# A two-layer encoder trunk on one core: the scaling of the turned queries, two units later in the written order

## The chip, the cores and the metric

The kernel runs on one core of one Trainium2 chip. The metric is the device time of one execution in microseconds; a kernel is run several times and the median counts. One execution is also recorded by the hardware profiler, and that record is the trace that is read here.

## What is computed

The trunk has a batch of 1, 256 rows (frames), a width of 2048, 16 heads of 128 and two layers, all in float32. The part around the change is layer a's attention. Cut to that, the reference reads:

```python
u = rms_norm(h, a_norm_g[l])
proj = u @ a_w_in[l]                                   # 2048 -> 3*2048 + 16
q, k, v, fz = jnp.split(proj, [D, 2 * D, 3 * D], axis=-1)
q = rms_norm(q.reshape(B, S, H, Dh), a_q_g[l])
k = rms_norm(k.reshape(B, S, H, Dh), a_k_g[l])
logf = jax.nn.log_sigmoid(fz + a_b_f[l])
o = forgetting_attention(q, k, v, logf)                # causal softmax with a decay bias
h = h + o.reshape(B, S, D) @ a_w_out[l]
h = h + sq_relu_mlp(h, mlp_norm_g[layer], mlp_w1[layer], mlp_w2[layer])
```

A shared key and value projection, a second layer with chunked attention (layer b) and a second MLP follow.

## The kernel before

Every large product is made of units. A unit takes a weight tile of 128 x 1024 numbers, which ScalarE (ACT) and VectorE (DVE) split in two: line 339 writes the high part `hi`, line 340 the rest `lo`. TensorE (PE) then does three passes: `hi` with the high part of the activations (line 608), `hi` with their low part (line 610) and `lo` with the high part (line 612). Weights come either as loaded tiles (`raw`, line 310, and the tiles called `R`, `h` and `w`) or as sums of two of them (`wT`), since pairs of panels share seven products in place of eight. Some pairs of layer a are 1536 columns wide; the 512 that are over are split into `half` by the same two lines. A `hi` tile has three buffers, so ACT can be at most a few units ahead of PE.

The projection of layer a runs by four groups g of four heads: queries, keys and values of a group one after the other. When the query panel of a group is done, its rows are normed and turned, so that a head's 128 numbers lie across the partitions:

- `head_norm` (line 666): ACT squares (676), DVE sums (679, 683), POOL takes the power -1/2 (684), ACT scales the rows by it (`qn`, 690) and DVE transposes blocks of 32 x 32 into `z` (456).
- `carry` (line 459): one DMA writes `z` to DRAM (`turn`, 466), four DMAs read it back with blocks exchanged (472). For the queries of the second to fourth group POOL issues the four; for the keys SP issues them, into the half tile called `R`.
- `scale_q` (line 708): one ACT instruction (711) reads the landed tile (`z`, 128 x 1024), multiplies by a gain for each partition and writes `q` in the layout that the scores use.

The keys go the same way without the last step. `attend` (783) then puts the softmax of each head into the order: scores on PE (744, 745: `po<-R,q`), exponentials on ACT (757), the probabilities turned through DRAM (`pbuf`), values on PE (776, 777), and the result split by ACT (780) and DVE (781).

What comes when on an engine is set by the order in which the program is written. `keep_order` chains the instructions of each engine in the written order, and each engine takes them strictly in turn. Work beside the units stands in a queue, `fill`: `add_fill` appends a list of items, one slot for each coming unit, and `run_fill` executes one slot, mostly once for each unit (a table of masks says 0, 1 or 2). An empty list in front of an item so puts it one slot later. `of_q` is called once for each group when the query panel is finished, and adds `scale_q` that many slots behind.

Words in the rows: `acc` and `s` are pairs of PSUM tiles; line 1042 and line 1052 copy or negate one of them on ACT between the forms of a pair (`p<-s`, `s<-s`), and line 1046 copies another; line 990 makes a summed weight tile on DVE; line 1005 adds one weight tile to another by a DMA from POOL.

Of the kernel before, what the change touches and what calls it, by code (L numbers as in the profile page):

```python
# [102 lines left out]
def trunk(ctx: ExitStack, tc: tile.TileContext, xT, xr, gs, hg, bf, wgate, w_in, w_in3, w_ins, w_oa, w1a, w1fa, w1sa, w2fa, w2sa,  # L103
# [340 lines left out]
    def steps(make):  # L444
        box = []

        def step():
            if not box:
                box.append(make())
            next(box[0])  # L450
        return step
# [34 lines left out]
    def turned(name=None):  # L486
        z = qkv.tile([P, GH * T], F32, name="z")
        return (z, qkv.tile([P, GH * T], F32, name=name, tag=name, bufs=2)) if name else z
# [177 lines left out]
    def head_norm(stats, z, dst, late=0, apart=None, reader=SY):  # L666

        rest = []

        def f(b, ps):  # L670
            sq = wk.tile([P, 512], F32, name="sq", tag="wk")
            ss = sm.tile([P, 3 * GH], F32, name="ss")
            rn = ss[:, GH : 2 * GH]

            def square():
                S.activation(sq, ps, AF.Square)

            def total():
                V.tensor_reduce(ss[:, :GH], sq.rearrange("p (a d) -> p a d", a=GH), axis=AX.X, op=ALU.add)

            def norm():
                vv = ss[:, 2 * GH :]
                V.tensor_scalar(vv, ss[:, :GH], 1.0 / P, stats().e[:, b : b + 1], op0=ALU.mult, op1=ALU.add)
                G.tensor_tensor(rn, vv, mhalf, op=ALU.pow)

            def turn():
                qn = wk.tile([P, 512], F32, name="qn", tag="wk")
                for a in range(GH):
                    c = slice(a * P, a * P + P)
                    S.activation(qn[:, c], ps[:, c], AF.Copy, scale=rn[:, a : a + 1])  # L690
                blocks32(qn, z, b)

            if apart is None:
                square()
            rest.append((square, total, norm, turn))
            if b == NB - 1:
                turns = [[t] for _, _, _, t in rest] + carry(z, dst, 1, reader)
                if apart is not None:
                    add_fill([[]] * apart + [[s, t, n] for s, t, n, _ in rest] + turns)
                    return  # L700
                for _, total, norm, _ in rest:
                    total()
                    if not late:
                        norm()
                add_fill([[]] * (late - 1) + ([[n for _, _, n, _ in rest]] if late else []) + turns)
        return f

    def scale_q(land, layer, g):
        tag = "qs"[g // 2 if layer else 0]
        q = qkv.tile([P, GH, T], F32, name="q", tag=tag, bufs=2)  # L710
        S.activation(q.rearrange("p a (b i c) -> p (a b) i c", b=NB, i=4),
                     land.rearrange("p (i ab c) -> p ab i c", i=4, c=32), AF.Copy, scale=gqk[:, layer : layer + 1])
        return q
# [56 lines left out]
    def free(g):  # L770
        assert g < 2 or set(range(g * GH - 2 * GH, g * GH - GH)) <= served, "rooms in use"
# [11 lines left out]
    def attend(g, q, k, v, decay, o, make_bias):  # L783
        st = [{} for _ in range(GH)]
        box = {}
        k4 = k.rearrange("p (i a b c) -> p a b i c", i=4, a=GH, b=NB)
        *at, far = TABLES["ATA" if decay else "ATB"][g]
        items = [[] for _ in range(at[-1] + far + 1)]
        step = steps(lambda: make_bias(g, box))
        for i in (5, 8, 9) if decay and g == 0 else (3, 6, 7):  # L790
            items[i].append(step)
        for a in range(GH):
            step = steps(lambda a=a: softmax(st[a], g, a, q(), k4, box["b"]))
            for i in range(4):
                items[at[a] + i].append(step)
            items[at[a] + 3].append(lambda a=a: add_fill(st[a]["carry"]))
            items[at[a] + far].append(lambda a=a: values(st[a], a, v, o, g * GH + a))
        return items

    def v_evac(v, r):  # L800
        def f(b, ps):
            S.activation(v[:, b, :], ps, AF.Copy, scale=r[:, b : b + 1])
        return f

    def add_fill(items):
        for i, it in enumerate(items):
            if i < len(fill):
                fill[i] = fill[i] + it
            else:
                fill.append(it)  # L810
# [29 lines left out]
    def rows_in(i):  # L840
        here.add(i)
        b, n = chunks[2 * i]
        c = slice(n * 512, n * 512 + UN)
        SY.dma_start(h[b][:, c], xr[b][:, c])
# [164 lines left out]
    def prepare(p, d):  # L1009
        if d == p.units[1] and "11 half" in p.has:  # L1010
            p.has.remove("11 half")
            SY.dma_start(p.t["11"][:, UN : p.cols], p.big["11"][:, UN : p.cols])
        if p.deep and d == p.units[4] - 1:
            make(p, "T3", 1)
        for name, at in zip(("12", "22", "21", "11", "T3", "T1"), p.units):
            if d == at and p.deep and name == "T3":
                make(p, "T3", 0)
            elif d == at:
                (bring if name[0] != "T" else put if p.adds and name == "T1" else make)(p, name)
# [117 lines left out]
    def sub(tag):  # L1137
        if tag not in halves_of:
            halves_of[tag] = room(tag, "R")
        return halves_of[tag]  # L1140
# [45 lines left out]
    def heads(out):  # L1186
        o, fs, qs, vs = [None] * H, [], {}, {}

        def of_q(g):
            box = []  # L1190

            def f(b, ps):
                if b == 0:
                    z, lq = turned("z")
                    box.extend((head_norm(lambda: st0, z, lq, 0 if g else 6, None, G if g else SY), lq))
                box[0](b, ps)
                if b == NB - 1:
                    add_fill([[]] * (7 + (0 if g else 6)) + [[lambda: qs.update({g: scale_q(box[1], 0, g)})]])
            return f

        def of_k(g):
            box = []

            def f(b, ps):
                if b == 0:
                    free(g)
                    box.append(sub(f"k{g % 2}")[:, : GH * T])
                    box.append(head_norm(lambda: st0, turned(), box[0]))
                    vs[g] = sub(f"v{g % 2}")[:, :UN].rearrange("p (b c) -> p b c", b=NB)
                box[1](b, ps)  # L1210
                if b == NB - 1:
                    add_fill(attend(g, lambda: qs[g], box[0], vs[g], True, o, decay_bias))
            return f

        def of_v(g):
            return lambda b, ps: v_evac(vs[g], st0.r)(b, ps)

        evacs = [f(g) for g in range(NG) for f in (of_q, of_k, of_v)]
        box = [13]

        def after():
            prepare(plan_h[0][0], box[0])
            box[0] -= 1

        panels(x, evacs[:1], begin, after)
        step = steps(head_gains)
        add_fill([[step], [], [], [], [step]])
        add_fill([[lambda: rows_in(3)]])
        add_fill([[lambda i=i: enter(i)] for i in range(8 - TABLES["RI"][3], 8)])
        fill[TABLES["RI"][3] - 1].append(st0.roots)  # L1230
        add_fill([[]] * TABLES["GS"][0] + gates(x, st0))
        step = steps(lambda: sum_x(fs))
        for i in TABLES["XS"]:
            add_fill([[]] * i + [[step]])
        panels(x, evacs[1:2], None, after, tail=tail_h)
        base = turns[0]

        last = next(p for p, q, i in plan_h[::-1] if isinstance(p, Pair) and p.order == "three")
        step3 = steps(lambda: sum_third(x, fs))
        add_fill([[]] * TABLES["X3"] + [[step3]] * 4)  # L1240
        run(plan_h, opener(x, fs, evacs, o, out, base, last, TABLES["XOH"], True), TABLES["HM"], plan_a[0][0])
        halves_of.clear()
        owner.clear()
# [21 lines left out]
    qs, evs = [], []  # L1265
    for g in range(NG):
        box = {}

        def f(b, ps, box=box, g=g):
            if b == 0:  # L1270
                z, lq = turned("z")
                box["lq"], box["f"] = lq, head_norm(lambda: st2, z, lq, apart=0 if g else None)
            box["f"](b, ps)
            if b == NB - 1:
                add_fill([[]] * (9 if g else 7) + [[lambda: qs.append(scale_q(box["lq"], 1, g))]])
# [146 lines left out]
```

## Time and profile before

| | |
|---|---|
| three runs | median 2060.13 us (2053.63 to 2060.47) |
| the profiled execution | 2058.26 us, of which the span of the trace is 2056.5 us |
| granted TensorE clock | 1.000 over the span |
| PE busy | 2044.3 us (99%) |
| DVE, ACT, POOL busy | 1784.8, 1409.1, 259.6 us |
| DMA | 560.92 MB, mean 273 GB/s |

The span is what the trace covers; 1.8 us of the execution lie around it. Busy time of PE is nearly the whole span, so what can be saved without leaving work out is the time in which PE stands still or follows late. An idle time in brackets in a timeline row stands ahead of that row's instruction on its engine, and the name behind the arrow is what it waited for.

### The profile page before, as it was taken

Reading aid. Unit: us, or ns where it says so; the run is one execution under the profiler, and the core shown is the slowest. Engines: PE = TensorE matmul, PEld = TensorE weight load, DVE = VectorE, ACT = ScalarE, POOL = GpSimd, SP = SyncE. Lnnn points to the kernel's source line nnn. Section 1 sums busy time; section 2 is a strip of 40 time slices with the busy share of each in tenths; the row PEclk is TensorE's granted clock in tenths of the full one; section 3 lists DMA queues with packets and bytes.
Section 4 is the critical chain, followed back from the end, with each engine's and each line's share of the span. In section 5 each row is a group of like instructions: output and inputs, shape, how many; then the busy total and the mean of one; then the engine's idle time right before and its main releaser. Section 6 shows DMA issues by size and latency. Waiting matters only on the chain.

```text
span 2056.5 us, 27163 instructions
## 1 busy us (share of the span) xinstructions
PE 2044.3 (99%) x9048; PEld 1684.9 (82%) x9048; DVE 1784.8 (87%) x2099; ACT 1409.1 (69%) x1826; POOL 259.6 (13%) x371
## 2 busy tenths in 40 slices
PE   9999999999999999999999999999999999999999
PEld 8778878878888888888888888888888888888887
DVE  7788887899899899899888788889988988988996
ACT  7666666677676677676778666667766676776764
POOL 1122110021101102101012111100111111111020
PEclk9999999999999999999999999999999999999999
DMA  8898998898888898898989988888988888888985
GB/s 324 268 286 268 303 294 243 296 280 259 295 265 278 262 296 277 235 291 274 263 252 290 290 256 273 262 267 280 291 290 259 272 265 297 254 288 257 299 260 150
DMA packets 176749, 560.92 MB, mean 273 GB/s; under 512 B 40912, under 2 KB 67936, under 8 KB 154080
## 3 DMA queue, kind: packets, MB, share of 16 engines
q1 hardware_dynamic: 153824, 464.47, 64.0%
q0 software_dynamic: 22496, 94.42, 23.5%
q8 instruction: 71, 1.16, 0.2%
q14 instruction: 70, 0.57, 0.1%
q10 hardware_dynamic: 288, 0.30, 0.0%
HBM read 519.22 MB, written 27.29 MB: 266 GB/s over the span
## 4 chain that ended last, share of the span: by engine, by line
PE 88%; DMA 5%; DVE 3%; issue 2%; ACT 2%; POOL 0%; SPq 0%; ACTq 0%; DVEq 0%; POOLq 0%
PE acc L612 21%; PE acc L608 21%; PE acc L610 21%; PE s L612 8%; PE s L608 8%; PE s L610 8%; DVE lo L340 1%; ACT hi L339 1%; PE po L745 1%; DMA z<-turn 1%; DMA w<-in_w2fa 1%; PE po L776 1%; DMA wT<-in_w1fb 1%; DMA raw<-in_w_ins 0%; DMA q<-z 0%
## 5 line engine op out<-in xcount | busy, mean ns | idle before, releaser
L340 DVE TENSOR_TENSOR lo<-raw,hi 128x1024 fp32r<-128x1024 f32 (+1 forms) x401 | 485.2, 1214 | 80.3 <-ACT hi L339 73.6
L339 ACT ACTIVATE hi<-raw 128x1024 fp32r<-128x1024 f32 (+1 forms) x401 | 420.9, 1053 | 193.6 <-PE acc L610 121.9
L608 PE MATMUL acc<-hi,act 128*128 128x512 f32 x1750 | 490.3, 393 | 0.5 <-ACT hi L339 0.2
L612 PE MATMUL acc<-lo,act 128*128 128x512 f32 x1750 | 485.0, 390 | 1.1 <-DVE lo L340 1.0
L610 PE MATMUL acc<-hi,act 128*128 128x512 f32 x1750 | 484.2, 389 | 0.0
L612 PEld LDWEIGHTS acc<-lo,act 128*128 128x128 f32 x1750 | 327.6, 188 | 73.0 <-DVE lo L340 5.2
L610 PEld LDWEIGHTS acc<-hi,act 128*128 128x128 f32 x1750 | 328.4, 188 | 69.1 <-DVE act L399 0.4
L608 PEld LDWEIGHTS acc<-hi,act 128*128 128x128 f32 x1750 | 326.6, 188 | 68.8 <-ACT hi L339 2.2
L339 ACT ACTIVATE hi<-w 128x1024 fp32r<-128x1024 f32 x254 | 266.6, 1057 | 122.8 <-PE acc L610 82.5
L340 DVE TENSOR_TENSOR lo<-wT,hi 128x1024 fp32r<-128x1024 f32 x220 | 266.9, 1220 | 64.6 <-ACT hi L339 60.9
L340 DVE TENSOR_TENSOR lo<-w,hi 128x1024 fp32r<-128x1024 f32 x254 | 305.3, 1217 | 16.0 <-ACT hi L339 14.5
L339 ACT ACTIVATE hi<-wT 128x1024 fp32r<-128x1024 f32 x220 | 231.9, 1060 | 103.1 <-PE acc L610 44.3
L608 PE MATMUL s<-hi,act 128*128 128x512 f32 x522 | 144.6, 392 | 2.3 <-ACT hi L339 2.3
L612 PE MATMUL s<-lo,act 128*128 128x512 f32 x522 | 143.2, 389 | 0.1
L610 PE MATMUL s<-hi,act 128*128 128x512 f32 x522 | 142.7, 388 | 0.0
L482 POOL DMA_DIRECT2D q<-z x192 | 95.6, 508 | 253.1 <-DVE z L456 211.3
L608 PEld LDWEIGHTS s<-hi,act 128*128 128x128 f32 x522 | 97.5, 188 | 23.4 <-ACT hi L339 3.5
L612 PEld LDWEIGHTS s<-lo,act 128*128 128x128 f32 x522 | 97.4, 188 | 21.7 <-DVE lo L340 1.9
L610 PEld LDWEIGHTS s<-hi,act 128*128 128x128 f32 x522 | 97.9, 188 | 20.4
L608 PE MATMUL s<-hi,S 128*128 128x512 f32 x288 | 89.0, 390 | 0.0
L612 PE MATMUL s<-lo,S 128*128 128x512 f32 x288 | 88.8, 389 | 0.3 <-DVE lo L340 0.3
L610 PE MATMUL s<-hi,S 128*128 128x512 f32 x288 | 88.7, 389 | 0.0
(247 smaller groups left out, 2384.6 us busy)
## 6 DMA issues: line engine op xcount, KB each, us to landing
w<-in_w2fa SPq DMA_DIRECT2D x32, 1024.0 KB, 6.2
w<-in_w2fb SPq DMA_DIRECT2D x32, 1024.0 KB, 6.5
w<-in_w1fa SPq DMA_DIRECT2D x27, 1024.0 KB, 7.3
w<-in_w1fb SPq DMA_DIRECT2D x27, 1024.0 KB, 7.4
raw<-in_w2sa SPq DMA_DIRECT2D x52, 512.0 KB, 8.1
raw<-in_w2sb SPq DMA_DIRECT2D x50, 512.0 KB, 7.4
raw<-in_w_kv SPq DMA_DIRECT2D x48, 512.0 KB, 5.5
raw<-in_w1sb SPq DMA_DIRECT2D x46, 512.0 KB, 6.7
```

The costliest lines, as they stand in the source:

```text
L339: S.activation(hi[:, c], raw[:, c], AF.Copy)
L340: V.tensor_tensor(lo[:, c], raw[:, c], hi[:, c].bitcast(F32), op=ALU.subtract)
L482: (G if i % 2 else SY).dma_start(dst[32 * j : 32 * j + 32, i * n : (i + 1) * n], z[32 * i : 32 * i + 32, j * n : (j + 1) * n])
L608: TE.matmul(ps[:, cols], xh, cut(hi, j), start=first, stop=False, **kw)
L610: TE.matmul(ps[:, cols], xl, cut(hi, j), start=False, stop=False, **kw)
L612: TE.matmul(ps[:, cols], xh, cut(lo, j), start=False, stop=last, **kw)
L745: TE.matmul(s[:, P : 3 * P], q[:, a, P:T], k[:, a], start=True, stop=True)
L776: TE.matmul(po[:, :T], v[:, 0, a * P : (a + 1) * P], pT[:, :2], start=True, stop=False)
```

## The change

One number in `of_q`: the scaling of the queries goes into the ninth slot behind the end of the panel in place of the seventh, for the second to fourth group. The first group stays at 13. Nothing is added or removed, and layer b is not touched.

```diff
                 if b == NB - 1:
-                    add_fill([[]] * (7 + (0 if g else 6)) + [[lambda: qs.update({g: scale_q(box[1], 0, g)})]])
+                    add_fill([[]] * (9 if g else 13) + [[lambda: qs.update({g: scale_q(box[1], 0, g)})]])
             return f
```

On PE, POOL and SP the written order is the same as before; on DVE only names differ. On ACT three rows move, L711 once for each of the three groups. At the second group, ACT before (the row of L711 stands right behind the high part of a summed weight tile `wT`, ahead of that tile's `half`):

```order
L339 ACTIVATE hi<-wT_1286 128x1024
L711 ACTIVATE q<-z,gqk 128x1024
L339 ACTIVATE half<-wT_1286 128x512
L339 ACTIVATE hi<-raw 128x1024
L1042 ACTIVATE p_1448<-s 128x512
L339 ACTIVATE hi<-wT_1286 128x1024
L1052 ACTIVATE s<-s 128x512
L780 ACTIVATE act<-po 128x256
L339 ACTIVATE half<-wT_1286 128x512
```

ACT now, in the same place of the second group:

```order
L339 ACTIVATE hi<-wT_1286 128x1024
L339 ACTIVATE half<-wT_1286 128x512
L339 ACTIVATE hi<-raw 128x1024
L1042 ACTIVATE p_1446<-s 128x512
L339 ACTIVATE hi<-wT_1286 128x1024
L1052 ACTIVATE s<-s 128x512
L780 ACTIVATE act<-po 128x256
L711 ACTIVATE q<-z,gqk 128x1024
L339 ACTIVATE half<-wT_1286 128x512
```

L711 has moved behind six instructions and now stands ahead of the `half` of the next summed tile. At the third group it moves in the same way, from ahead of the two `qn` of the keys to behind them and the `hi<-wT` that follows. At the fourth group, ACT before (here `sq` and `qn` belong to the norm of the keys):

```order
L418 ACTIVATE S<-sum 128x512 x2
L711 ACTIVATE q<-z,gqk 128x1024
L676 ACTIVATE sq<-acc 128x512 x2
L339 ACTIVATE hi<-R 128x1024
L690 ACTIVATE qn<-acc,ss 128x128 x4
L339 ACTIVATE hi<-raw 128x1024
L780 ACTIVATE act<-po 128x256
L690 ACTIVATE qn<-acc,ss 128x128 x4
L339 ACTIVATE hi<-wT_2447 128x1024
```

ACT now, in the same place of the fourth group:

```order
L418 ACTIVATE S<-sum 128x512 x2
L676 ACTIVATE sq<-acc 128x512 x2
L339 ACTIVATE hi<-R 128x1024
L690 ACTIVATE qn<-acc,ss 128x128 x4
L339 ACTIVATE hi<-raw 128x1024
L780 ACTIVATE act<-po 128x256
L711 ACTIVATE q<-z,gqk 128x1024
L690 ACTIVATE qn<-acc,ss 128x128 x4
L339 ACTIVATE hi<-wT_2447 128x1024
```

The squares, the first `qn` and the `hi` of a loaded tile now stand ahead of L711; the second `qn` stands behind it.

## The prediction

> **What bounds the kernel now.** I read the page's first and fourth parts, then who waited for whom over the whole span.
>
> ```profile
> span 2056.5 us, 27163 instructions
> PE 2044.3 (99%) x9048; PEld 1684.9 (82%) x9048; DVE 1784.8 (87%) x2099; ACT 1409.1 (69%) x1826; POOL 259.6 (13%) x371
> PE 88%; DMA 5%; DVE 3%; issue 2%; ACT 2%; POOL 0%; SPq 0%; ACTq 0%; DVEq 0%; POOLq 0%
> ```
>
> PE stands still for 2056.5 - 2044.3 = 12.2 us in all. A change that leaves every product in place can win little more than that, 0.6% of the span, and only what belongs to its own three places. The waits of ACT and PE (total, times, longest):
>
> ```profile
> ACT q L711 <- DMA z<-turn: 9.5, 4, 4.0
> PE s L608 <- ACT half L339: 1.7, 1, 1.7
> PE po L744 <- DMA R<-turn: 0.8, 1, 0.8
> ```
>
> L711 is the scaling. ACT waits for its turned tile four times of eight. The second row is the one long stop of PE behind a `half`; the third comes back below. So I went to the places of the scaling in the timeline (start, duration, instruction, idle time before it and its releaser). Second group:
>
> ```profile
> 130.08 2.84 POOL L472 DMA_DIRECT2D z<-turn  x4
> ...
> 142.57 0.61 PE L612 MATMUL s<-lo,S 128*128 128x512 f32 x2
> ...
> 143.21 1.15 ACT L711 ACTIVATE q<-z,gqk 128x1024 f32<-128x1024 f32 x1 [4.00 <-DMA z<-turn]
> ...
> 144.27 0.61 ACT L339 ACTIVATE half<-wT 128x512 fp32r<-128x512 f32 x1
> ...
> 144.93 0.50 PE L608 MATMUL s<-half,S 128*128 128x512 f32 x1 [1.75 <-ACT half L339]
> ...
> 146.20 0.60 ACT L1042 ACTIVATE p<-s 128x512 f32<-128x512 f32 x1 [0.37 <-PE s L612]
> ...
> 148.53 1.20 PE L612 MATMUL acc<-lo,act 128*128 128x512 f32 x4
> 148.58 0.62 ACT L339 ACTIVATE half<-wT 128x512 fp32r<-128x512 f32 x1
> ...
> 149.87 0.68 DVE L340 TENSOR_TENSOR half<-wT,half 128x512 fp32r<-128x512 f32 x1
> ...
> 150.71 0.19 PEld L608 LDWEIGHTS s<-half,S 128*128 128x128 f32 x1
> ```
>
> POOL issues the four reads of the turned tile from 130.08 us on, they land at about 143.1, ACT is held from 139.2, and `half<-wT`, which stands behind the scaling, comes so late that PE stops. The windows around it (length, busy time of PE, PEld, DVE, ACT, POOL, granted clock, DMA share, GB/s):
>
> ```profile
> 143.20:149.75 6.55, 4.82 (x20) 3.61 (x21) 4.84 (x6) 6.13 (x9) 0.00 (x0) 1.00 0.80 286
> 192.00:196.00 4.00, 4.00 (x20) 3.25 (x19) 3.43 (x8) 4.00 (x10) 1.66 (x3) 1.00 0.52 171
> 217.00:221.00 4.00, 4.00 (x19) 3.34 (x18) 2.94 (x4) 3.55 (x4) 0.21 (x1) 1.00 0.66 227
> 203.00:208.00 5.00, 5.00 (x25) 4.20 (x24) 4.88 (x8) 3.78 (x8) 4.06 (x4) 1.00 1.06 268
> 271.00:288.00 17.00, 16.18 (x70) 12.05 (x69) 14.90 (x22) 13.71 (x25) 5.14 (x5) 1.00 0.79 241
> ```
>
> The clock is at 1.00 in all of them, so the stop costs its own length and no slower matmuls behind it.
>
> **The change, second group.** What the stop costs is more than the 1.75 us of idle time, since PE follows late for some instructions more. From the end of `s<-lo` (142.57 + 0.61 = 143.18) to the end of the unit at 148.53 (149.72 with the 1.20 us of that row, rounded) PE does 19 matmuls: three on `half`, four of 256 and 128 columns, twelve of 512. The chain shows an undisturbed stretch of the same 19:
>
> ```profile
> 209.21 0.23 PE acc L608
> ...
> 212.62 0.43 PE po L776 x2
> 213.05 0.22 PE po L777 x2
> ```
>
> It goes from 209.21 to 213.05 + 0.22 = 213.27, 4.06 us. The same work took 6.54 us, so 2.48 us are lost here. [...]
>
> After the move `half<-wT` starts at about 139.2 and takes 0.61 us, so it is there 3 us before PE needs it, and the stop goes. ACT then waits at `p<-s` for PE (it did so before, 0.37 us), which ties it to PE again. From the start of `p<-s` to that of the next `half` it took 148.58 - 146.20 = 2.38 us; the scaling in between makes 3.53. PE needs that `half` at 150.71 - 146.20 = 4.51 us after `p<-s` (some 4.4 if the unit at 148.53 is no longer stretched), and it is done after 3.53 + 0.62 = 4.15: just in time on ACT. The DVE part, 0.68 us more, is done at 4.15 + 0.68 = 4.83 and wanted two matmuls of 0.23 later (the row at 209.21), at 4.4 + 0.46 = 4.86. That leaves nothing for the waking of one engine by another, so I take 0.2 us back. Second group: 2.48 - 0.2 = 2.3 us gained. The bounds: 2.48 if nothing comes back, and a whole scaling back, 2.48 - 1.15 = 1.3.
>
> The moved scaling comes after its data has landed: `p<-s` can start when `s<-half` is done, 143.18 + 0.68 = 143.9, and the scaling 2.38 later at 146.3, against 143.1. Its result is read first by the scores (L744; first and last start in each group):
>
> ```profile
> L744 PEld LDWEIGHTS po<-R,q x8: 187/188/188, 158.9 to 185.6; 128*128 128x128 f32 x8
> L744 PEld LDWEIGHTS po<-R,q x6: 187/188/188, 225.8 to 249.9; 128*128 128x128 f32 x6
> ```
>
> At 158.9 us, eleven after its end: nobody waits for it. No DMA moves, and no row on POOL or SP. The tile that the scaling reads is one of two, and the keys' `z` of the same group goes into the other one, so the later reading holds no writer up.
>
> **Third group.** ACT waits here too, and PE does not:
>
> ```profile
> 204.17 1.16 ACT L711 ACTIVATE q<-z,gqk 128x1024 f32<-128x1024 f32 x1 [2.21 <-DMA z<-turn]
> ...
> 213.31 0.38 ACT L780 ACTIVATE act<-po 128x256 fp32r<-128x256 f32 x1 [1.61 <-PE po L777]
> ```
>
> The window 203 to 208 has PE busy 5.00 of 5.00, so nothing is to be won. Moved, the 1.16 us fall ahead of a wait of 1.61 us of ACT for PE, which hides them; the scores read q only at 225.8. I take 0, between a loss of 1.16 (that cover gone) and a gain of 0.
>
> **Fourth group.** No wait at L711, but it stands ahead of the norm of the keys and of two splits that PE waits for:
>
> ```profile
> 272.39 1.13 ACT L711 ACTIVATE q<-z,gqk 128x1024 f32<-128x1024 f32 x1
> ...
> 277.03 0.73 PE L612 MATMUL acc<-lo,act 128*128 128x512 f32 x2 [0.29 <-DVE lo L340]
> ...
> 278.29 1.20 PE L608 MATMUL s<-hi,act 128*128 128x512 f32 x4 [0.53 <-ACT hi L339]
> 278.37 1.17 ACT L690 ACTIVATE qn<-acc,ss 128x128 f32<-128x128 f32 x4
> ...
> 281.33 0.34 SPq L466 DMA_DIRECT2D turn<-z  x1
> ...
> 294.35 0.46 PE L744 MATMUL po<-R,q 128*128 128x128 f32 x2 [0.80 <-DMA R<-turn]
> ```
>
> Without the 1.13 us in front the squares, the first `qn` and `hi<-raw` come about 1.1 us earlier, and the two stops, 0.29 + 0.53 = 0.82 us, go. Behind the second `qn` ACT is where it was, so `hi<-wT` and its `lo` are as late as before, and PE meets them sooner: I let 0.3 come back and take 0.5 us. Bounds: 0 (all comes back there) and 0.82 with the 0.80 at 294.35, 1.6.
>
> **The sum.** 2.3 + 0 + 0.5 = 2.8 us. The profiled execution took 2058.26 us; the forecast is 2058.26 - 2.8 = 2055.5 us. That execution lies inside the runs (2053.63 to 2060.47; all four together average 2058.1), 1.9 under their median. A measurement of this kernel tells about 0.5%, 10.3 us, from no change, so the gain is under that.
>
> **Rivals.** First, the gain is given back further down, because weights are no earlier than before. For it speaks the place where ACT waits for a load and PE starts on the result almost at once:
>
> ```profile
> 230.29 1.06 ACT L339 ACTIVATE hi<-raw 128x1024 fp32r<-128x1024 f32 x1 [2.98 <-DMA raw<-in_w_ins]
> ...
> 231.49 1.09 PE L608 MATMUL acc<-hi,act 128*128 128x512 f32 x4
> ```
>
> If that load keeps its hour, a PE that comes 2.3 us earlier waits 2.3 us here. Against it: the DMA engines paused at 192 to 196 (share 0.52) and 217 to 221 (0.66), where 4 x 0.48 + 4 x 0.34 = 3.3 us of their time were free, so they can move up with SP's issues. Then only the 0.5 us of the fourth group stay: 2058.26 - 0.5 = 2057.8.
>
> Second, on the other side, the keys' turn of the fourth group gets late. The second `qn` now stands behind the scaling, and from it runs `z`, `turn<-z`, `R<-turn` to the scores at 294.35, where PE already waits. If the squares do not come earlier (sums or POOL's power hold the first `qn`), the 0.5 us of this group are not won and the second `qn` is 1.13 us late. In a fuller DMA queue the keys' write may then take what it took in the second group, not what the queries' write of the fourth took:
>
> ```profile
> turn<-z SPq DMA_DIRECT2D x1, 512.0 KB, 6.5
> turn<-z SPq DMA_DIRECT2D x1, 512.0 KB, 4.3
> ```
>
> (in this order; the last number is us to landing). Price 1.1 + 2.2 = 3.3 us; it decides the sign as soon as it is over the 2.3 of the second group. Time: 2058.26 - 2.3 + 3.3 = 2059.3.
>
> Third, the wait follows the scaling. Loads that ACT and DVE release sooner could delay the four reads:
>
> ```profile
> z<-turn POOLq DMA_DIRECT2D x4, 128.0 KB, 11.4
> R<-turn SPq DMA_DIRECT2D x4, 128.0 KB, 2.6
> ```
>
> They took 11.4 us to land where the same reads on SP's queue took 2.6. They would have to land after 146.3, 3.2 us later than now; each us beyond is lost, since the next `half` is just in time. With 2 us of it, 2058.26 - 2.8 + 2 = 2057.5. Against it: all four were issued by 132.9, before anything has changed. [...]
>
> **How the numbers follow.** Forecast 0.60; given back 0.22; keys late 0.10; wait follows 0.08. None of the four leaves the 0.5% by itself: from 2.48 + 1.6 = 4.1 us gained (2054.2) to 1.0 lost (2059.3). The runs of one kernel lie up to 4.6 us under and 2.2 over the profiled one, and only together with such a spread could a median pass the bound: 0.03 faster, 0.95 same, 0.02 slower. The range: below, the forecast with the lowest run's distance, 2055.5 - 4.6 = 2050.9; above, the second rival with the highest run's, 2059.3 + 2.2 = 2061.5.
>
> **What would show it.** At the second group no stop of PE behind `half<-wT`, no wait at L711, and 19 matmuls in about 4.2 us; at the fourth `hi<-raw` about 1 us earlier relative to `S<-sum`; PE idle about 1.7 to 2.6 us less than 12.2 in all. A wait of over 4 us for `raw<-in_w_ins` with PE idle near 229 us would prove the first rival, a longer wait at L744 than 0.80 near 292 the second, an idle ahead of L711 the third. Wrong in kind I would be if time moved in the 1700 us behind 320 us, which the change does not touch.

## The result and the profile after

The changed kernel's median is 2054.24 us over 20 runs (2049.64 to 2057.40), and that of the kernel before, run beside it, 2057.07 us over 20 (2053.63 to 2062.18). The ratio is 0.9983, with a 95% interval of 0.9975 to 0.9990: 2.8 us by the medians, 2.1 to 5.1 us by the interval. It is a gain, and it is under the 0.5% that the prediction named. A second comparison, r5_after_again below, gave 0.9987 (0.9976 to 0.9998).

The profiled execution of the changed kernel took 2057.40 us, the longest of its 20. The page's first lines:

```profile
span 2055.6 us, 27163 instructions
...
PE 2044.0 (99%) x9048; PEld 1685.0 (82%) x9048; DVE 1786.1 (87%) x2099; ACT 1410.2 (69%) x1826; POOL 259.3 (13%) x371
```

PE stands still for 2055.6 - 2044.0 = 11.6 us, against 12.2 before. This pair of executions alone would show 0.9 us of span and 0.6 us of idle time; the table further down shows where the rest went. The waits of ACT and PE that answer to those shown of before (total, times, longest):

```profile
ACT q L711 <- DMA z<-turn: 0.4, 1, 0.4
PE po L776 <- DMA pbuf<-turn: 1.2, 1, 1.2
PE po L744 <- DMA R<-turn: 1.1, 1, 1.1
```

ACT's wait for the turned tile has gone from 9.5 us to 0.4, and what is left belongs to the first group, which the change does not move. PE's wait behind `half` is no longer in the list. A wait of 1.2 us that before did not have is: PE at L776, the values' product, for the probabilities' own turned tile. The timeline of the changed kernel, second group, then third, then fourth:

```profile
140.74 0.67 ACT L339 ACTIVATE half<-wT 128x512 fp32r<-128x512 f32 x1
...
143.14 0.61 PE L612 MATMUL s<-lo,S 128*128 128x512 f32 x2
143.60 0.39 PE L608 MATMUL s<-half,S 128*128 128x512 f32 x1
...
144.47 0.60 ACT L1042 ACTIVATE p<-s 128x512 f32<-128x512 f32 x1 [2.11 <-PE s L612]
...
145.64 0.67 PE L776 MATMUL po<-pbuf,R 128*128 128x256 f32 x2 [1.20 <-DMA pbuf<-turn]
...
146.85 1.14 ACT L711 ACTIVATE q<-z,gqk 128x1024 f32<-128x1024 f32 x1
147.89 0.62 ACT L339 ACTIVATE half<-wT 128x512 fp32r<-128x512 f32 x1
...
150.48 0.39 PE L608 MATMUL s<-half,S 128*128 128x512 f32 x1
...
210.85 1.18 ACT L711 ACTIVATE q<-z,gqk 128x1024 f32<-128x1024 f32 x1
...
270.16 1.15 ACT L418 ACTIVATE S<-sum 128x512 fp32r<-128x512 f32 x2 [0.54 <-DVE row L759]
...
274.95 1.08 ACT L339 ACTIVATE hi<-raw 128x1024 fp32r<-128x1024 f32 x1
...
276.16 1.18 ACT L711 ACTIVATE q<-z,gqk 128x1024 f32<-128x1024 f32 x1
277.20 1.16 ACT L690 ACTIVATE qn<-acc,ss 128x128 f32<-128x128 f32 x4
...
279.14 0.34 SPq L466 DMA_DIRECT2D turn<-z  x1
...
281.41 0.60 ACT L1042 ACTIVATE p<-acc 128x512 f32<-128x512 f32 x1 [1.15 <-PE acc L612]
...
292.84 0.46 PE L744 MATMUL po<-R,q 128*128 128x128 f32 x2 [1.12 <-DMA R<-turn]
```

In the second group `half<-wT` starts at 140.74, 2.9 us ahead of the matmul at 143.60 that reads it, and that matmul follows `s<-lo` without a gap. The scaling at 146.85 waits for nothing. The `half` behind it starts 147.89 - 144.47 = 3.42 us after `p<-s`, and PE reads it at 150.48 without a wait. But in between, PE stops at L776 for 1.20 us.

### The profile page after: what moved, and what is told of

Its sections match the earlier page's. It is cut to its first block, busy times and chain, and to the rows that moved or that the text cites. A ratio compares the mean times of both kernels' runs of the same rounds, so it can differ in the third digit from the quotient of the medians.

```text
span 2055.6 us, 27163 instructions
## 1 busy us (share of the span) xinstructions
PE 2044.0 (99%) x9048; PEld 1685.0 (82%) x9048; DVE 1786.1 (87%) x2099; ACT 1410.2 (69%) x1826; POOL 259.3 (13%) x371
## 4 chain that ended last, share of the span: by engine, by line
PE 90%; DMA 5%; DVE 2%; ACT 1%; issue 1%; SPq 0%; POOL 0%; DVEq 0%; ACTq 0%; POOLq 0%
PE acc L608 21%; PE acc L612 21%; PE acc L610 21%; PE s L612 8%; PE s L608 8%; PE s L610 8%; DVE lo L340 1%; DMA wT<-in_w1fb 1%; ACT hi L339 1%; PE po L745 1%; PE po L776 1%; DMA w<-in_w2fa 1%; DMA w<-in_w1fb 1%; DMA raw<-in_w_in 1%; DMA raw<-in_w_ins 0%
## 5 line engine op out<-in xcount | busy, mean ns | idle before, releaser
L608 PE MATMUL acc<-hi,act 128*128 128x512 f32 x1750 | 490.6, 393 | 0.4 <-ACT act L780 0.2
L608 PEld LDWEIGHTS acc<-hi,act 128*128 128x128 f32 x1750 | 326.4, 188 | 69.6 <-ACT hi L339 2.9
L608 PE MATMUL s<-hi,act 128*128 128x512 f32 x522 | 144.6, 392 | 0.3 <-ACT hi L339 0.3
L608 PEld LDWEIGHTS s<-hi,act 128*128 128x128 f32 x522 | 97.5, 188 | 21.5 <-ACT hi L339 1.6
L608 PE MATMUL s<-hi,S 128*128 128x512 f32 x288 | 89.1, 390 | 0.0
```

The costliest lines, as they stand in the source:

```text
L608: TE.matmul(ps[:, cols], xh, cut(hi, j), start=first, stop=False, **kw)
```

## The experiments

Most edits are to the list length in the line that queues the scaling (`g` counts the groups from 0; before, it is 13 for the first and 7 for the others; changed, 13 and 9).

**One part alone, and the opposite direction.** First the kernel before once more, unchanged.

> The kernel before, once more, for a second profile of it. Theory (the wait of ACT at the scaling of the second group is what the change removed): ACT waits at L711 again in the second and third group, for about 4 and 2 us, and PE stops behind half<-wT for 1 to 2 us near 145 us. Rival (the gain comes from elsewhere, and the wait of one profile was chance): the wait at L711 is under 1 us or PE does not stop there.

It took 2057.86 us. The stop is there again, 1.67 us long, and behind it something that the first execution did not have:

```profile
143.34 0.50 PE L608 MATMUL s<-half,S 128*128 128x512 f32 x1 [1.67 <-ACT half L339]
...
145.62 2.05 PE L608 MATMUL acc<-hi,act 128*128 128x512 f32 x4
```

Four matmuls of 512 columns take 2.05 us here. In the execution that the prediction read, the same four took 1.17:

```profile
146.57 1.17 PE L608 MATMUL acc<-hi,act 128*128 128x512 f32 x4
```

The windows behind the stop, of this execution and then of the first (length, busy time of PE, PEld, DVE, ACT, POOL, granted clock, DMA share, GB/s):

```profile
144.00:148.00 4.00, 4.00 (x12) 3.33 (x12) 4.00 (x6) 3.52 (x7) 0.00 (x0) 0.57 0.68 280
```

```profile
145.00:149.00 4.00, 4.00 (x17) 2.92 (x18) 4.00 (x5) 3.60 (x6) 0.00 (x0) 1.00 0.89 353
```

After the stop the granted clock was 0.57 for four microseconds, so 4.00 x 0.43 = 1.7 us of PE's time were lost on top of the 1.67 of the stop. In the first execution the clock stayed at 1.00.

The second group alone, and the third and fourth alone:

```
- add_fill([[]] * (7 + (0 if g else 6)) + [[lambda: qs.update({g: scale_q(box[1], 0, g)})]])
+ add_fill([[]] * (13, 9, 7, 7)[g] + [[lambda: qs.update({g: scale_q(box[1], 0, g)})]])     # r2
+ add_fill([[]] * (13, 7, 9, 9)[g] + [[lambda: qs.update({g: scale_q(box[1], 0, g)})]])     # r3
```

> Only the second group's scaling two units later; third and fourth stay in the seventh slot. Theory: no wait at L711 in the second group, no stop of PE behind half<-wT there, a wait of about 2 us of ACT in the third group that PE does not feel, and most of the gain: 2.3 of 2.8 us, so a ratio of 0.9988 and a median 2 to 3 us under before. Rival (the fourth group carries the gain): ratio 1.000.

> Only the third and fourth group's scaling two units later; the second stays in the seventh slot. Theory: the stop of PE behind half<-wT near 145 us is there as before, the two stops of PE near 277 and 278 us go, and the time falls by 0.5 us, which timing can hardly tell: ratio 0.9997, between 0.999 and 1.0005. Rival (the fourth group carries the gain): ratio 0.9985.

The second group alone gave a ratio of 0.9991 (0.9980 to 1.0002), the other two 1.0002 (0.9991 to 1.0013). By these times the parts cannot be told from nothing, nor from each other: each interval is over 4 us wide. The traces do tell. In r3 the stop behind `half` is there, 1.98 us long, and the granted clock over 144 to 150 us is 0.72, with 0.50 over 147 to 149 us, so it halved behind the stop here too (6.00 x 0.28 = 1.7 us); the two stops of the fourth group near 277 us are gone. In r2 the stop behind `half` is gone, and PE stops at L776 in its place. A timeline row of r3, then the timeline and a window of r2:

```profile
144.53 0.50 PE L608 MATMUL s<-half,S 128*128 128x512 f32 x1 [1.98 <-ACT half L339]
```

```profile
144.69 0.98 PE L776 MATMUL po<-pbuf,R 128*128 128x256 f32 x2 [2.12 <-DMA pbuf<-turn]
```

```profile
144.00:149.00 5.00, 4.31 (x13) 3.56 (x14) 2.35 (x3) 3.51 (x7) 0.97 (x1) 0.66 0.90 288
```

In this execution the new wait was as long as the old, and the clock fell behind it too, to 0.50 over 145 to 148 us (5.00 x 0.34 = 1.7 us).

Two units earlier than before:

```
+ add_fill([[]] * (5 if g else 13) + [[lambda: qs.update({g: scale_q(box[1], 0, g)})]])
```

> The same number turned the other way: fifth slot in place of the seventh for the second to fourth group. Theory (ACT waits at the scaling for the landing of the four reads, and what stands behind it makes PE stop): in the second group ACT is held from about 134.6 to 143 us, ahead of half<-h that PE wants at 138, so PE stops some 6 to 8 us there; in the third from about 196 to 204, 4 to 8 us of PE; in the fourth 0 to 3 us. In sum 10 to 18 us slower, ratio 1.005 to 1.009. Rival (the place of the scaling hardly matters, other work covers it): within 2 us of before.

Measured: 2067.0 us, ratio 1.0049 (1.0033 to 1.0066), so 10 us lost. The waits and a window of this kernel:

```profile
ACT q L711 <- DMA z<-turn: 19.2, 4, 9.9
...
PE s L608 <- ACT half L339: 9.0, 1, 9.0
```

```profile
140.00:150.00 10.00, 4.25 (x10) 3.26 (x11) 4.48 (x6) 7.00 (x14) 0.00 (x0) 0.51 0.54 173
```

The tile lands no earlier: ACT starts on it at 143.00 us, where it was 143.21 before. So ACT stands 9.9 us at the scaling in place of 4.0, and PE 9.0 us behind the `half` that comes after it in place of 1.75, as the theory wants. Most of the loss is in this one group; the third lost less than the 4 to 8 us that I had expected, with one stop of 1.90 us near 208 us.

**What takes the gain back.** The changed kernel again:

> The changed kernel once more, for a second profile and more runs. Theory A (as the profiles so far show it: in the second group the stop of PE behind half<-wT of 1.7 to 2.0 us gives way to a stop of 1.2 to 2.1 us at po L776, which waits for the turned probabilities pbuf<-turn): the stop at L776 is there again near 145 us, the two stops near 277 us are gone, ratio 0.9975 to 0.999. Rival B (the stop at L776 was chance, and the second group wins 2.3 us as forecast): no stop over 0.6 us of PE between 138 and 150 us.

2055.06 us, ratio 0.9987 (0.9976 to 0.9998). This execution has no stop in the second group at all: L776 finds its tile. Its windows there and its rows at the landmarks used below:

```profile
144.00:148.00 4.00, 4.00 (x21) 3.33 (x20) 1.88 (x3) 3.73 (x6) 0.61 (x1) 1.00 0.92 364
```

```profile
133.88 0.59 PE L776 MATMUL po<-pbuf,R 128*128 128x256 f32 x2
...
144.07 0.59 PE L776 MATMUL po<-pbuf,R 128*128 128x256 f32 x2
...
157.18 0.46 PE L744 MATMUL po<-R,q 128*128 128x128 f32 x2
...
229.49 1.06 ACT L339 ACTIVATE hi<-raw 128x1024 fp32r<-128x1024 f32 x1 [3.43 <-DMA raw<-in_w_ins]
230.60 1.21 PE L608 MATMUL acc<-hi,act 128*128 128x512 f32 x4 [0.76 <-ACT hi L339]
...
293.71 0.46 PE L744 MATMUL po<-R,q 128*128 128x128 f32 x2 [1.67 <-DMA R<-turn]
```

PE does 21 matmuls in 4.00 us without a gap. Having come early, it waits 0.76 us at 230 for a load, which is the place of the first rival, and 1.67 us at L744.

If the wait at L776 was what kept the gain small, it should pay to move the values of that head one unit later as well. The same edit on the kernel before is the control:

```
- items = [[] for _ in range(at[-1] + far + 1)]
+ items = [[] for _ in range(at[-1] + far + 2)]
- items[at[a] + far].append(lambda a=a: values(st[a], a, v, o, g * GH + a))
+ items[at[a] + far + (decay and (g, a) == (0, 3))].append(lambda a=a: values(st[a], a, v, o, g * GH + a))
```

> The change, and beside it the values of the last head of the first group (po L776, L777 and their split) one unit later, behind the twelve matmuls that follow them. Theory A (the probabilities land a little too late for a PE that no longer stops): no stop at L776 near 145 us, 1.2 to 2 us less than the changed kernel in the window of the second group, ratio to before 0.997 to 0.998. Rival B: nothing more than the change alone gives, ratio 0.9983.

> The kernel before with the values of the last head of the first group one unit later, and the scaling where it was. Theory A: nothing won, since the stop of 1.7 to 2.0 us behind half<-wT stays and PE comes to L776 after the probabilities have landed anyway: ratio 0.9995 to 1.0005. Rival B': the later values win by themselves, 1 to 2 us, ratio 0.9991 to 0.9995.

With the change: 2055.24 us, ratio 0.9992 (0.9982 to 1.0003). On the kernel before: 2057.79 us, ratio 1.000 (0.999 to 1.001). The wait at L776 was gone in r6, and the time was no better than the changed kernel's. Its trace, of the longest of its twelve executions (2061.29 us), has a longer wait further down instead: PE waits 2.00 us for the load near 230 us, and the clock is at 0.50 over 234 to 236 us behind that. Whether this is the price of the edit or chance, one trace does not tell:

```profile
233.77 2.03 PE L608 MATMUL acc<-hi,act 128*128 128x512 f32 x4 [2.00 <-ACT hi L339]
```

In r7 the stop behind `half` stayed, 2.53 us, and the clock did not fall behind it; a timeline row and a window:

```profile
144.25 0.50 PE L608 MATMUL s<-half,S 128*128 128x512 f32 x1 [2.53 <-ACT half L339]
```

```profile
144.00:148.00 4.00, 3.20 (x12) 2.07 (x13) 3.77 (x5) 3.60 (x6) 0.00 (x0) 1.00 0.89 317
```

Is ACT short of time at the new place? r8 does the scaling twice in the second to fourth group, with the same result, so ACT has 1.15 us more to do there:

```
+ for _ in range(2 if layer == 0 and g else 1):
      S.activation(q.rearrange("p a (b i c) -> p (a b) i c", b=NB, i=4), ...
```

> The changed kernel with the scaling of the second to fourth group done twice in a row, 3 x 1.15 us more of ACT. Theory (the moved scaling has cover in the second and third group and is on the keys' way in the fourth): no new stop of PE in the second and third group, and at the fourth the scores at L744 wait 1.2 us longer for R<-turn than in the changed kernel (1.1 there, so about 2.3). Rival (the moved scaling stands on PE's way in each group): a stop of about 1 us more behind half<-wT or hi in the second and third group as well.

One execution, 2053.24 us. In the third group PE goes on without a gap. In the second no stop of PE is listed, but PE's loads of the `half` behind the two scalings (PEld) come late:

```profile
147.35 0.19 PEld L608 LDWEIGHTS s<-half,S 128*128 128x128 f32 x1 [0.55 <-ACT half L339]
...
148.08 0.19 PEld L612 LDWEIGHTS s<-half,S 128*128 128x128 f32 x1 [0.43 <-DVE half L340]
```

From the start of `s<-lo` to that of the product behind the `half` PE takes 148.42 - 146.62 = 1.80 us, against 149.51 - 148.38 = 1.13 in r5. So 0.67 of the 1.15 us show on PE, and only about 0.5 us were covered. In the fourth group one stop appeared, ahead of the product behind the splits:

```profile
279.59 0.73 PE L608 MATMUL acc<-hi,S 128*128 128x512 f32 x2 [1.16 <-ACT hi L339]
```

The longer wait at L744 that I had expected did not come; there was none at all in this execution, although the second `qn` was behind two scalings. So in this execution the wait at L744 did not follow `qn` one for one.

**The keys of the fourth group, and the spread.** r9 puts the fourth group's scaling behind the second `qn`, so that the keys' turn starts a scaling earlier:

```
+ add_fill([[]] * (13, 9, 9, 12)[g] + [[lambda: qs.update({g: scale_q(box[1], 0, g)})]])
```

> The change, with the fourth group's scaling in the twelfth slot in place of the ninth: behind the second qn of the keys and the next two hi<-wT. Theory (in the changed kernel the scaling of the fourth group delays the keys' turn by its own 1.15 us, and the scores at L744 wait 1.1 to 1.7 us for it): the wait at L744 falls by about 1.1 us, the stretch of the fourth group is about 1 us shorter than in the changed kernel, ratio to before 0.9975 to 0.9985. Rival (the turn lands when the DMA queues let it, whatever ACT does): the wait at L744 stays between 1.1 and 1.8 us, ratio as the changed kernel's.

2055.58 us, ratio 0.9990 (0.9978 to 1.0001). Its timeline:

```profile
269.82 1.15 ACT L418 ACTIVATE S<-sum 128x512 fp32r<-128x512 f32 x2 [0.54 <-DVE row L759]
...
275.82 1.17 ACT L690 ACTIVATE qn<-acc,ss 128x128 f32<-128x128 f32 x4
...
292.23 0.46 PE L744 MATMUL po<-R,q 128*128 128x128 f32 x2 [1.25 <-DMA R<-turn]
```

`qn` comes 6.00 us after `S<-sum` (7.04 in the changed kernel), yet L744 still waits 1.25 us. So in this trace the wait at L744 did not follow how early ACT does `qn`.

Then one more execution of each kernel, to see how far executions of the same program differ:

> The kernel before, a third profile. Theory: a stop of PE behind half<-wT of 1.7 to 2.7 us near 141 to 145 us, as in all four executions in which the second group's scaling is in its old place; from the 125th to the 320th microsecond (by matmuls) PE needs 195 to 198 us. Rival (the differences between executions are as large as the change): no such stop.

> The changed kernel, a third profile. Theory: no stop behind half<-wT; PE either goes on or stops at L776 for the probabilities; where it goes on, the second group's stretch is 3.5 us shorter and 1 to 1.8 us of that come back at the load near 229 us. The same stretch as in r10 takes 193.5 to 195 us. Rival: 195 to 198 as before.

2059.77 and 2055.89 us. The third execution of before had the longest stop of all, and the clock down for seven microseconds behind it; timeline and window:

```profile
131.94 0.59 PE L776 MATMUL po<-pbuf,R 128*128 128x256 f32 x2
...
145.44 0.79 PE L608 MATMUL s<-half,S 128*128 128x512 f32 x1 [3.82 <-ACT half L339]
...
161.98 0.38 PE L744 MATMUL po<-R,q 128*128 128x128 f32 x2
```

```profile
145.00:152.00 7.00, 6.56 (x17) 5.23 (x18) 6.58 (x8) 5.88 (x10) 1.54 (x2) 0.54 0.62 194
```

Last, three units more than the change:

```
+ add_fill([[]] * (12 if g else 13) + [[lambda: qs.update({g: scale_q(box[1], 0, g)})]])
```

> The scaling of the second to fourth group in the twelfth slot, five units later than before in place of two. Theory (only that it comes after its data has landed counts): as the changed kernel in the second and third group, and at the fourth as r9; ratio 0.997 to 0.999. Rival (two units are a best place, and later the scaling meets other work that PE waits for): a stop of PE of about 1 us in the second or third group that the changed kernel does not have, ratio 0.9985 to 1.000.

2054.79 us, ratio 0.9990 (0.9975 to 1.0004). The second group is as good as in r5 and no better (23.37 us between the landmarks A and B explained below, where r5 has 23.30). In the fourth PE waits 1.82 us at L776 (274.33 us) and 3.29 us at L744 (294.17 us) in this execution, and the clock is at 0.50 over 296 to 298 us behind the second of these.

No version tried is shown to be faster than the changed kernel.

**Where the time went.** PE's matmuls stand in the same order in both kernels, so the time between the same two matmuls can be compared over executions. Three executions of each kernel, in us; A is the values of the third head in the first group (L776 near 133), B the first scores of the second group (L744 near 159), C the product behind the load near 231 (L608, four matmuls), D the scores of the fourth group (L744 near 294). Each number is the difference of two starts in the timeline, as the rows of r5 and r10 above and these of before and after, with those at B and C of both:

```profile
133.50 0.59 PE L776 MATMUL po<-pbuf,R 128*128 128x256 f32 x2
...
159.10 0.38 PE L744 MATMUL po<-R,q 128*128 128x128 f32 x2
```

```profile
133.82 0.59 PE L776 MATMUL po<-pbuf,R 128*128 128x256 f32 x2
...
158.64 0.38 PE L744 MATMUL po<-R,q 128*128 128x128 f32 x2
...
231.01 1.07 PE L608 MATMUL acc<-hi,act 128*128 128x512 f32 x4
```

| execution | start to A | A to B | B to C | C to D | D to end | A to D | span |
|---|---|---|---|---|---|---|---|
| before | 133.50 | 25.60 | 72.39 | 62.86 | 1762.15 | 160.85 | 2056.5 |
| before, r1 | 131.99 | 26.96 | 73.14 | 63.78 | 1760.23 | 163.88 | 2056.1 |
| before, r10 | 131.94 | 30.04 | 72.40 | 62.69 | 1760.93 | 165.13 | 2058.0 |
| changed | 133.82 | 24.82 | 72.37 | 61.83 | 1762.76 | 159.02 | 2055.6 |
| changed, r5 | 133.88 | 23.30 | 73.42 | 63.11 | 1761.49 | 159.83 | 2055.2 |
| changed, r11 | 132.93 | 23.68 | 73.28 | 63.18 | 1761.03 | 160.14 | 2054.1 |
| mean changed minus mean before | +1.07 | -3.60 | +0.38 | -0.40 | +0.66 | -3.62 | -1.90 |

Three more traces have the second group's scaling at one of the two places and nothing else changed from A to B. By the starts of the same two rows r3, at the old place, took 160.12 - 132.87 = 27.25 us. At the new place r2 took 159.32 - 132.21 = 27.11, with its stop of 2.12 us at L776 and the half clock behind it, and r9 took 156.29 - 131.95 = 24.34, with a stop of 0.97 us there. With them the means from A to B are 27.46 us (four executions) and 24.65 (five), a gain of 2.81 us in place of 3.60. The two ranges, 25.60 to 30.04 and 23.30 to 27.11 us, overlap, so that the size of this gain is known to about 1 us only (an estimate from these spreads). From B to C the same nine give 72.58 and 73.35 us, so 0.77 us come back there.

From A to D, where the change acts, 3.6 us are gone in the six executions of the table, within the interval of the ratio. Ahead of A nothing differs between the kernels, and behind D only what comes from earlier; those stretches differ by up to 2 us between executions of one program, and in these six they happened to go against the change by 1.07 + 0.66 = 1.7 us. In the first pair of profiles A to D fell by 160.85 - 159.02 = 1.83 us, with the wait of 1.20 us at L776 in it, and the rest grew by 0.32 + 0.61 = 0.93; that is why this pair showed 0.9 us.

## Why the prediction was right, and where its sizes were off

The forecast was 2.8 us gained on an execution of 2058.26; measured are 2.8 by the medians and 3.5 by the ratio (0.0017 x 2058), most of it in the second group, as forecast. That 2.8 met 2.8 is luck in part: the interval is 2.1 to 5.1 us, and of two things that the sum left out, the half clock behind the old stop (0.50 in r1, r3 and r10) adds to the gain and the wait at L776 (1.20 us in the profiled execution) takes from it. The time itself came out 1.3 us under the forecast of 2055.5, since the execution read for it was 1.2 us over the median of the 20 of before (2057.07). Point by point:

**Second group, forecast 2.3 of a loss of 2.48.** The stop behind `half<-wT` is in all five traces with the scaling at its old place (1.67 to 3.82 us) and in none of the eight with it later; two units earlier it is 9.0 us. For the execution that the prediction read the loss was right: A to B took 25.60 us there and 23.30 in r5, which has no stop, so 2.30 us. As a term for the kernel it does not hold from one execution to the next: the mean gain from A to B is 3.60 us in the six executions of the table and 2.81 in the nine, both over the upper bound of 2.48, though by no more than their spread. The step that failed is the sentence "so the stop costs its own length and no slower matmuls behind it". It was read from one execution, where the clock stayed at 1.00. In r1, r3 and r10 the clock was at 0.50 for some microseconds behind the stop: r1 lost 26.96 - 23.30 = 3.66 us, of which 1.67 are the stop and 1.7 the clock. And the stop's length is not fixed: ACT waited 3.9 us for the tile in r1, 4.0 in the profiled execution and 5.9 in r10.

Read microsecond by microsecond, the clock is at 0.50 over 145 to 147 us in r1, over 147 to 149 in r3 and over 145 to 151 in r10, behind stops of 1.67, 1.98 and 3.82 us. It is at 1.00 throughout from 140 to 150 us in the first execution of before, with its stop of 1.75 us, and in r7, with one of 2.53. So the length of the stop alone did not decide it: 1.67 us were enough in r1, and 2.53 us in r7 were not. What did decide is not shown.

**0.2 us back in the second group.** `half` was just in time as worked out (3.42 us after `p<-s`, forecast 3.53), and r8 shows about 0.5 us more room than I gave it. The 0.2 us were my estimate, and no run shows them as a term of their own. What does come back there I had not seen at all: the wait at L776 for `pbuf<-turn`, 1.20 us in the profiled execution, 2.12 in r2, 0.97 in r9, 0.32 in r11, none in r5, r8 and r12. The four traces with the old stop and the values in their place do not have it: it seems that the old stop had covered it, and that PE coming early meets the next transfer that is late. So the forecast of 19 matmuls in about 4.2 us holds where that tile is there in time (4.08 us in r5, from 143.39 to 147.47), and not in the profiled execution.

**Third group, forecast 0.** Right: the window from 203 to 208 us already had PE busy for 5.00 of 5.00 and has it so now, the wait of ACT of 2.21 us is gone, and PE shows nothing for it.

**Fourth group, forecast 0.5.** The two stops of 0.29 and 0.53 us are gone, and `hi<-raw` starts 274.95 - 270.16 = 4.79 us after `S<-sum`, against 5.82 before, so 1.0 us earlier as forecast. The rows of before that this is measured against:

```profile
271.34 1.15 ACT L418 ACTIVATE S<-sum 128x512 fp32r<-128x512 f32 x2 [0.54 <-DVE row L759]
...
277.16 1.08 ACT L339 ACTIVATE hi<-raw 128x1024 fp32r<-128x1024 f32 x1
...
283.23 0.60 ACT L1042 ACTIVATE p<-acc 128x512 f32<-128x512 f32 x1 [1.80 <-PE acc L612]
```

From `S<-sum` to `p<-acc`, which follows PE, it was 11.89 us in each of the three executions of before and is 11.25 in each of the three of the changed kernel, so 0.64 us are gained up to there. The mean from C to D fell by 0.40. The rest seems to come back at L744 and not, as I had it, behind the later splits: the waits there are 0.80, 1.66 and 1.30 us before, 1.12, 1.67 and 1.75 after, 0.26 more in the mean, which is less than they differ among themselves.

**The rivals.** The gain given back near 230 us was the best of them, and a part of it is real: B to C is 0.38 us longer in the mean of the six executions and 0.77 in that of the nine, with a wait of 0.76 in r5. It is not the whole: had the load kept its hour, B to C would have grown by all that A to B lost. The second rival priced a late keys' turn at 3.3 us. SP issues the keys' write 279.14 - 270.16 = 8.98 us after `S<-sum` where it was 9.99 before, so it is earlier, and in r9 the wait at L744 did not follow ACT's order. The third did not occur: the moved scalings of the second to fourth group wait for nothing in the three traces of the changed kernel.

**PE's idle time, forecast 1.7 to 2.6 us less than 12.2.** It fell by 0.6 in the profiled execution, so this sign of it was missed. Over three executions each it is 12.2, 12.4 and 13.6 us before and 11.6, 11.4 and 11.3 after, 1.3 less in the mean. In the profiled pair the wait at L776 took 1.20 us of it, and a wait far behind the change, at 878 us, was 1.23 us long where it had been 0.43. In r1 and r10 the slower matmuls behind the stop count as busy (in r1 PE is busy for 4.00 of the 4.00 us at a clock of 0.57, with 12 matmuls where the first execution has 17), so that there idle time leaves out a part of what the old stop cost.

Still open is why the clock fell behind one stop of about 1.7 us (1.67 in r1) and not behind another (1.75 in the first execution of before), why the turned tiles land up to 2 us apart (for `z<-turn`, ACT's wait in the second group ended 9.63 to 11.78 us after A in the three executions of before; for `pbuf<-turn`, PE's wait ended 11.82 us after A in the profiled execution of the changed kernel and 10.68 in r11), and whether r6, r9 and r12 differ from the changed kernel at all: their intervals overlap its own.

## What to carry to other kernels

Here one instruction that waited 4.0 us for a transfer held up what stands behind it on its engine, and PE stopped for 1.75 us. Such an instruction belongs where its data has landed and its reader is still far; before counting the gain, look for the next late transfer that the old stop was covering (here up to 2.12 us at L776). Price a stop of PE over several executions, with the granted clock behind it: the stop of 1.7 us here cost 2.3 us in one execution and 3.7 in another. A gain of a thousandth is read from the time between the same two instructions, over a few traces of each kernel, and not from one pair of spans.

## What the runs showed of the hardware

The granted clock of PE fell to 0.50 behind single stops of 1.67 us (r1, over 145 to 147 us), 1.98 (r3, 147 to 149), 2.12 (r2, 145 to 148) and 3.82 us (r10, 145 to 151), and stayed at 1.00 behind stops of 1.75 (before) and 2.53 us (r7). I had expected the same stop to cost the same each time. Executions of one program on one core also differ: the first 133 us, untouched by any edit, took 131.9 to 133.9 us in the six executions of the table, and ACT's wait for the turned tile of the second group was 3.9 to 5.9 us in the three of before.
